# A transformer block's values stage: sums on one engine, stores and loads at other steps, and another split order in the gate pairs

## The chip, the cores and the metric

The kernel runs on one core of one Trainium2 chip. Its time is the device time of one execution in microseconds (us), the median of three runs, with the lowest and the highest beside it. Times of single instructions come from one profiled execution of the same program, which has a time of its own.

The engines are named as in the profile: PE is TensorE's matmul, PEld its weight load, DVE VectorE, ACT ScalarE, POOL GpSimd, and SP the engine that issues most DMAs. ACT and POOL issue DMAs as well, each in the order of its own instructions.

## The reference, cut to what matters

One layer on a residual stream x of 512 tokens by 2048 channels, with 8 attention heads and 8 retention heads of 128 channels each:

```python
h = rmsnorm(x, norm_gain)
proj = h @ w_in
(aq, ak, av, az, iq, ik, iw, rq, rk, rv, rz, ga, gb) = jnp.split(proj, SPLIT_POINTS, axis=-1)
...
a_out = dsa_mixer(aq, ak, av, iq, ik, iw, positions, rel_bias) * jax.nn.silu(az)
...
b_out = retention_mixer(rq, rk, rv, ret_gn_gain) * jax.nn.silu(rz)
merged = jax.nn.sigmoid(ga) * (a_out @ w_a_out) + jax.nn.sigmoid(gb) * (b_out @ w_b_out)
r = x + merged @ w_o
return r + (p_i @ w_ple) * jax.nn.sigmoid(r @ w_ple_gate)
```

The final RMSNorm follows. In `dsa_mixer` an indexer (iq, ik, iw) scores all earlier keys for each token, the 128 best are kept, and softmax attention runs over them with a bias that depends on the distance of two positions. `retention_mixer` rotates rq and rk by position, forms decayed scores within chunks, carries a state from chunk to chunk and normalizes each head. The product of h with w_in is most of the work; its columns are av, rv (1024 each), ga, gb (2048 each), and so on.

## The kernel before, in words

**Numbers in two parts.** The matmuls run in float32r. A weight tile of 128 x 1024 (`wraw`, `wt`) is cut into a high part `wh` (a copy by ACT, line 153, `split_to`) and a low part `wl = wraw - wh` (a subtraction by DVE, line 158). `split_to` queues the ACT copy at once and the subtraction `lag` steps later. Raw tiles are loaded by SP (`load_to`, line 132), some steps earlier. Where a product needs a sum of two weight blocks, a second DMA adds one block onto the raw tile; GpSimd issues it (`add_block`, line 119): for a tile in `in_big` (name `wt`, the attention values' sums) 12 steps after its load, and, for an add that follows a split, right after that split's subtraction. `wh` and `wl` have a few buffers each and `wraw` more, so a split waits for the matmuls that read the buffer's former contents.

**The order of the work.** The kernel writes the instruction order out by hand. After every second or third matmul it calls `step()` (line 181). Each call counts one step, runs what was put off until then by `later(n, f)` (line 175), then one entry of `todo`, or, if that is empty and the step number divides by `state["rate"]`, one entry of the list `bg`. `BG_RATES` (line 1394) gives the rate stage by stage: 2, 3, 5, 24, 16, 8. Every engine takes its instructions in this order, so an ACT instruction that waits holds all later ones of ACT.

**Stages**, in order: norm, rope tables and the indexer's products; the retention values (two calls of `values`, line 744); the attention values (`values_pair`, line 908); then for each head one pair of products for retention (`gate_pair` with `retention(h)`, line 772) and two gate pairs; then pairs for rz, aq and ak, az; at the end attention, the projections, merge and output.

**Seven products in place of eight.** A pair multiplies a 2 x 2 arrangement of blocks by seven products whose inputs are sums of blocks (Strassen's scheme in Winograd's form). `combos` (line 291) makes the seven left inputs from the normalized x, once, for each k from 0 to 7: `sums` (lines 310 to 317) forms four sums of 256 columns, and `parts` (line 297) writes the high part of an input into the left half of a tile (`LO`, ACT) and the low part into its right half (`HI`, line 301, or line 303 where the sign is turned). It is called as `Xh` with `adder` and three of the `low` parts on GpSimd. These calls, the loads and the norm of x (`xn_load`, `xn_norm`, lines 700 and 705) are entries of `bg`; they run while the indexer and the retention values are multiplied. Twelve of the input tiles (`x_away`: the last three products for k below 4) are stored to memory and loaded back in the second call of `values` (`x_load`, line 883, one load for each k from 4 on). The top-k's 48 rounds (line 647), the bias masks (line 659) and the bias products (line 669) are the entries that follow in `bg`; the result of a bias product is copied by ACT and stored from SP, 8 + 4n steps later (`bias_out`, line 689).

**A pair** (`gemm_pair`, line 236) has four PSUM banks p, v, q, r and 14 runs of eight matmuls, high parts over 512 columns and low parts over 256, with a step after every second matmul, so 56 steps. `SPLIT_AT` (line 233) tells ahead of which run which unit (weight tile) of this or the next pair is split; the entry 2: 4 has lag 5, the others 1. The seven units of a pair are, by `block_pair` (line 90), t, w11, w21, w22, t, t, w11; the fifth to seventh use tiles again, after an add.

**Retention.** When the pair's query half and then its key half are done, `rotate(i, o)` (line 783) copies the two halves of `o` into `rb`, swapped (ACT, lines 786 and 787), and multiplies and adds on DVE 3, 5 and 7 steps later; after the keys all further steps of the head are queued, 9 to 94 steps later (lines 875 to 878).

**Values.** `values` accumulates four PSUM tiles of 128 tokens; when they are done, ACT scales each into `rv` (line 764) and stores it (line 892). `values_pair` runs seven products of 16 steps. Its results: ACT copies PSUM to `pv`, `e1`, `e2`, `e3` (`copy`), and `value_out` (line 896) forms a sum `a` on DVE, its high part (ACT) and low part (DVE) two and three steps later, and stores both from ACT's queue 10 and 12 steps later (line 906). After the seventh product `last()` (line 921) calls this for four results at once.

Buffers: 69 tiles of 128 x 512 (`U`), and 5 big ones of 128 x 1280 (`B`: `wt`, `go`, masks).

Of the kernel before, what the change touches and what calls it, by code (L numbers as in the profile page):

```python
# [17 lines left out]
L = 512  # L18
# [17 lines left out]
def block_kernel(tc, xT, pT, posb, posq, w_in, w_v, w_ik, w_a, w_b, w_o, w_ple, w_gate,  # L36
# [4 lines left out]
    with contextlib.ExitStack() as ctx:  # L41
# [29 lines left out]
        raw_tiles = {}  # L71
        unfinished = {}
        state = {"raw": 0, "split": 0, "rate": BG_RATE}
        in_raws, in_big = set(), set()

        def raw(src, k0, nk, cols, plus=None):
            raws.append((src, k0, nk, cols, plus))
# [60 lines left out]
        def split_to(n, lag=1):  # L138
            while state["split"] < min(n, len(units)):
                i = state["split"]  # L140
                load_to(i + 1)
                r, plus, nk, cols = units[i]
                if r in unfinished:
                    unfinished[r]()
                raw = view(raw_tiles[r], nk, cols)
                if i in in_raws:
                    t = wp.tile([128, 2, 512], F32R, name="whl", tag="wraw", bufs=RAW_BUFS)
                    h, l = t[:, 0:1], t[:, 1:2]
                elif nk * cols == L:
# [3 lines left out]
                act.activation(h, raw, AF.Copy)  # L153

                def rest(r=r, plus=plus, l=l, raw=raw, h=h):
                    if unfinished.pop(r, None) is None:
                        return
                    dve.tensor_sub(l, raw, h.bitcast(F32))  # L158
# [71 lines left out]
                for n in ns]  # L230
        RUNS = [(n, part % 2) for n, part in RUNS]

        SPLIT_AT = {0: 3, 2: 4, 3: 4, 4: 5, 7: 6, 8: 7, 10: 8, 12: 9}
        LOAD_AT = (0, 2, 4, 6, 8, 10, 12)

        def gemm_pair(ids, X, done, late=False):
# [35 lines left out]
            for at, (n, part, ks) in enumerate(runs):  # L272
                at = max(at - 4, 0) if late else at
                i, o = ids[n], banks[n]
                if at in SPLIT_AT and not (late and at == 2):
                    split_to(ids[0] + SPLIT_AT[at], 5 if at == 2 else 1)
                if at in LOAD_AT:
                    load_to(ids[LOAD_AT.index(at)] + AHEAD + LOADS)
                w, c = loaded[i][part], (ALL, LO)[part]
                first = ended[n] == 0  # L280
                for k in ks:
                    ended[n] += 1
                    pe.matmul(o[:, c], w[:, k], X[PRODUCTS[n]][k][:, c], start=(n < 4 and first and k == 0),  # L283
                              stop=(ended[n] == 16), skip_group_check=True)
# [6 lines left out]
        def combos(lo, hi, name, keep=None, adder=dve, low={}):  # L291


            X = {n: [None] * 8 for n in PRODUCTS}
# [2 lines left out]
            def parts(n, k, src, sign=1.0):  # L297
                t = U(name + n, F32R)
                act.activation(t[:, LO], src, AF.Copy, scale=sign)
                if sign > 0:  # L300
                    low.get(n, dve).tensor_sub(t[:, HI], src, t[:, LO].bitcast(F32))
                else:
                    dve.scalar_tensor_tensor(t[:, HI], src, sign, t[:, LO].bitcast(F32), op0=OP.mult, op1=OP.subtract)
                dst = keep and keep(n, k)
# [5 lines left out]
            def sums(k):  # L310
                x, y = lo(k), hi(k)
                t1, t2 = T[k] = U("t1"), U("t2")
                adder.tensor_sub(t2[:, LO], x[:, LO], x[:, HI])
                adder.tensor_sub(t1[:, LO], x[:, HI], y[:, HI])
                adder.tensor_sub(t1[:, HI], x[:, LO], t1[:, LO])
                adder.tensor_sub(t2[:, HI], y[:, LO], t1[:, HI])

            def one(k, i):
                if i == 0:
# [302 lines left out]
        def index_tile(m, ix):  # L622
            if m > 1:
                todo.extend(N3)
            for s in range(2):
                for t in range(1, NT):
                    todo.append(lambda s=s, t=t: index_score(2 * m + s, ix[s], t))

        for m in range(2):
            index_tile(m, ix[m])  # L630
        for m in range(2, 8):
# [49 lines left out]
        def bias_out(b, ps):  # L681
# [4 lines left out]
            for n, g in enumerate(gs):  # L686
                dst = bass.AP(tensor=scr.tensor, offset=scr.offset + 16 * (g % 8) * 1280 + TOFF[t],
                              ap=[[1280, 16], [128 * 1280, NH], [1, ln]])
                later(8 + 4 * n, lambda dst=dst, n=n: sp.dma_start(dst, e[:, ln * n:ln * n + ln]))
# [5 lines left out]
        x_away = [(n, k) for k in range(X_AWAY) for n in PRODUCTS[4:]]  # L695
        hd = dp.tile([len(x_away), 128, L], F32, name="hd")
        x_at = {nk: hd[i] for i, nk in enumerate(x_away)}
        xn = {}

        def xn_load(k):  # L700
            for i in (k, k + 8):
                xn[i] = U("xn")
                sp.dma_start(xn[i], xT[:, i, :])

        def xn_norm(k):
            for i in (k, k + 8):
                dve.scalar_tensor_tensor(xn[i], xn[i], ng[:, i:i + 1], R["b"], op0=OP.mult, op1=OP.mult)

        Xh, h_step = combos(lambda k: xn[k], lambda k: xn[k + 8], "h", lambda n, k: x_at.get((n, k)), pool,
                            {n: pool for n in ("s1", "s4", "a22")})  # L710
        bg.append(lambda: xn_load(0))
        for k in range(8):
            if k < 7:
                bg.append(lambda k=k: xn_load(k + 1))
            bg.append(lambda k=k: xn_norm(k))
            bg.extend([lambda k=k, i=i: h_step(k, i) for i in range(X_STEPS)])

        bg.append(lambda: state.update(rate=BG_RATES[1]))
        for r in range(16):
            for t in range(1, NT):  # L720
                bg.append(lambda r=r, t=t: topk_round(t, r == 15))
# [50 lines left out]
        def retention(h):  # L772
# [22 lines left out]
            def queries():  # L795
                E["qt"] = U("qt")
# [84 lines left out]
        x_wanted = collections.deque(x_away)  # L881

        def x_load(s):
            if s >= KT - len(x_away) and x_wanted:
                n, k = x_wanted.popleft()
                Xh[n][k] = U("h" + n, F32R)
                sp.dma_start(Xh[n][k].bitcast(F32), x_at[n, k])

        for i in range(2):
            pss = values(u_rv[i], "rv", x_load if i else lambda s: None)  # L890
            for t, ps in enumerate(pss):
                act.dma_start(rd[i, t], normal(ps, "rv", t))
        state["rate"] = BG_RATES[2]


        def value_out(i, t, f, x, y):

            a = U("av")
            f(a, x, y)
            if t == NT - 1:  # L900
                vs = [(6, a)]
            else:
                h, l = split(a, "av", 2)
                vs = [(2 * t, h.bitcast(F32)), (2 * t + 1, l.bitcast(F32))]
            for j, v in vs:
                later(10 + 2 * (j % 2), lambda j=j, v=v: act.dma_start(vd[i, j], v))

        def values_pair(ids):
            banks = {}
# [4 lines left out]
                for j in range(2):  # L914
                    act.activation(E[n][j], banks[b][j], AF.Copy)

            def out(f, b, n, i, half):
                for j in range(2):
                    value_out(i, 2 * half + j, f, banks[b][j], E[n][j])
# [14 lines left out]
            for n, b in enumerate("vpqrpvp"):  # L934
# [3 lines left out]
                for s, (i, k) in enumerate(seq):  # L938
                    if k == 0:
                        split_to(i + AHEAD)  # L940
                        load_to(i + AHEAD + LOADS)
                    h, l = loaded[i]
                    x = Xh[PRODUCTS[n]][s]
                    for j in range(2):
# [7 lines left out]
                    after[n]()  # L952

        values_pair(u_av)
        state["rate"] = BG_RATES[3]


        sgb, sga, mbs = (dp.tile([16, 128, L], F32, name=n) for n in ("sgb", "sga", "mbs"))
# [26 lines left out]
        state["rate"] = BG_RATES[5]  # L985
        for n, u in enumerate(u_rz):
            y = B("y2")

# [402 lines left out]
AHEAD = 3  # L1391
LOADS = 5
BG_RATE = 4
BG_RATES = (2, 3, 5, 24, 16, 8)
X_AWAY = 4
HEAD = 13
WARM = 10
MANUAL = True
# [96 lines left out]
```

## Time and profile before

| | us |
|---|---|
| time, median of three runs | 1684.4 |
| lowest and highest of the three | 1682.68, 1685.42 |
| the profiled execution's own time | 1680.43 |
| its span in the trace | 1678.7 |

The profile's lines have these forms. A group has line, engine, operation, output<-inputs with partitions x elements and type, then the count, the busy time, the mean in ns of one, and the idle time of the engine ahead of them with what ended most of it. A wait has engine, tile and line, then what released it, with the idle time, the count and the longest. A stretch (`A:B`) has its length, then for PE, PEld, DVE, ACT and POOL the busy time with the number of instructions, then the clock granted to TensorE (1 is full), the share of time the DMA engines were busy, and GB/s. A line of the timeline has the start, the duration, engine, line, operation, tile and count, and in brackets the idle time before it with the releaser. ACTq and SPq mark DMA issues in an engine's queue; SP's issue line gives minimum, median and maximum in ns. The DMA table's last numbers are the count, the size of one and the median time from issue to landing.

### The profile page before, as it was taken

To read this page: it belongs to the slowest core of one execution; us is meant where nothing else is said; L and a number is where in the kernel's file an instruction comes from. 1 tells how busy PE (TensorE), PEld (TensorE's weight loads), DVE (VectorE), ACT (ScalarE), POOL (GpSimd) and SP (SyncE) were. 2 spreads that over 40 slices of the span, in tenths; PEclk is the share of its full clock that TensorE was granted. 3 is DMA by queue.
4 is the path that set the end of the run, shared out by engine and by line. 5 is a ranking of instruction groups with operands and counts; after the bars stand their busy time and mean duration, and the time that the engine had idled before them with its cause. 6 is when DMAs were issued, how large, how long until landed. Compare 5 with 4: busy or idle time off the path is not lost.

```text
span 1678.7 us, 24639 instructions
## 1 busy us (share of the span) xinstructions
PE 1660.2 (99%) x9160; PEld 1441.5 (86%) x9160; DVE 1300.1 (77%) x1984; ACT 880.0 (52%) x1296; POOL 284.3 (17%) x288
## 2 busy tenths in 40 slices
PE   9999999999999999999999999999999999999997
PEld 7988788888888888888888888888888888888896
DVE  7798988988988887887887777787668887864453
ACT  7465544555555555555555555566633445463342
POOL 2116611111111111111331111100000111112222
PEclk9999999999999999999999999999999999999999
DMA  7427989788788788788998888898466788733222
GB/s 288 127 91 236 321 234 268 174 218 218 181 210 220 178 232 230 168 229 227 248 235 219 218 223 218 247 373 284 162 210 193 196 216 218 208 108 101 88 63 101
DMA packets 125577, 343.26 MB, mean 204 GB/s; under 512 B 13713, under 2 KB 25873, under 8 KB 125457
## 3 DMA queue, kind: packets, MB, share of 16 engines
q1 hardware_dynamic: 90400, 235.22, 41.5%
q0 software_dynamic: 23680, 85.99, 28.1%
q10 hardware_dynamic: 11376, 20.47, 3.4%
q8 instruction: 72, 1.18, 0.3%
q14 instruction: 49, 0.39, 0.1%
HBM read 300.21 MB, written 41.42 MB: 204 GB/s over the span
## 4 chain that ended last, share of the span: by engine, by line
PE 89%; DVE 4%; ACT 2%; issue 2%; POOL 2%; DMA 1%; ACTq 0%; SPq 0%; POOLq 0%; DVEq 0%
PE ps_p L283 23%; PE ps_v L283 15%; PE ps_r L283 8%; PE ps_q L283 7%; PE ps_w L213 3%; PE ps_w L214 3%; PE ps_w L215 3%; PE ps_pg L215 3%; PE ps_pg L213 3%; PE ps_pg L214 3%; PE ps_iq L213 1%; PE ps_iq L215 1%; PE ps_iq L214 1%; DVE wl L158 1%; ACT wh L153 1%
## 5 line engine op out<-in xcount | busy, mean ns | idle before, releaser
L158 DVE TENSOR_TENSOR wl<-wraw,wh 128x1024 fp32r<-128x1024 f32 (+2 forms) x459 | 565.4, 1241 | 156.6 <-ACT wh L153 155.4
L153 ACT ACTIVATE wh<-wraw 128x1024 fp32r<-128x1024 f32 (+2 forms) x459 | 474.3, 1043 | 257.9 <-DVE wraw L160 120.3
L119 POOL DMA_DIRECT2D wraw<-w_in x120 | 106.1, 962 | 644.1 <-DVE mk L666 245.3
L283 PE MATMUL ps_p<-hs,wh 128*128 128x512 f32 x640 | 161.1, 394 | 0.0
L246 ACT ACTIVATE e<-ps_p 128x512 f32<-128x512 f32 x144 | 86.1, 598 | 136.7 <-PE ps_p L283 134.3
L283 PEld LDWEIGHTS ps_p<-hs,wh 128*128 128x128 f32 x640 | 114.9, 189 | 21.3 <-issue 0.7
L283 PE MATMUL ps_p<-hs,wl 128*128 128x256 f32 x640 | 92.1, 284 | 1.6 <-DVE wl L158 1.6
L283 PEld LDWEIGHTS ps_p<-hs,wl 128*128 128x128 f32 x640 | 83.0, 192 | 2.1 <-DVE wl L158 2.0
L283 PE MATMUL ps_r<-hs,wh 128*128 128x512 f32 x320 | 79.9, 392 | 1.3 <-ACT wh L153 1.3
L119 POOL DMA_DIRECT2D wraw<-w_o x24 | 21.1, 945 | 348.5 <-DVE wl L158 316.5
L283 PE MATMUL ps_q<-ha,wh 128*128 128x512 f32 x320 | 80.1, 392 | 0.0
L283 PE MATMUL ps_v<-ha,wh 128*128 128x512 f32 x320 | 80.0, 392 | 0.0
L283 PE MATMUL ps_p<-ha,wh 128*128 128x512 f32 x320 | 79.3, 390 | 0.0
L283 PE MATMUL ps_v<-hs,wh 128*128 128x512 f32 x320 | 79.0, 389 | 0.0
L215 PE MATMUL ps_pg<-rh,wl 128*128 128x512 f32 x192 | 74.8, 390 | 0.0
L214 PE MATMUL ps_pg<-rl,wh 128*128 128x512 f32 x192 | 74.7, 389 | 0.0
L213 PE MATMUL ps_pg<-rh,wh 128*128 128x512 f32 x192 | 74.7, 389 | 0.0
L967 DVE TENSOR_TENSOR go<-e_t 128x256 f32<-128x256 f32 x160 | 68.0, 425 | 6.8 <-DMA bd<-go 1.2
L283 PEld LDWEIGHTS ps_r<-hs,wh 128*128 128x128 f32 x320 | 59.6, 188 | 15.8 <-ACT wh L153 2.9
L283 PEld LDWEIGHTS ps_p<-ha,wh 128*128 128x128 f32 x320 | 59.9, 188 | 12.9 <-issue 0.5
L283 PEld LDWEIGHTS ps_v<-hs,wh 128*128 128x128 f32 x320 | 60.1, 188 | 12.5
L283 PEld LDWEIGHTS ps_v<-ha,wh 128*128 128x128 f32 x320 | 59.5, 188 | 12.1
(409 smaller groups left out, 3739.9 us busy)
## 6 DMA issues: line engine op xcount, KB each, us to landing
wraw<-w_in SPq DMA_DIRECT2D x172, 512.0 KB, 5.3
wraw<-w_in POOLq DMA_DIRECT2D x120, 512.0 KB, 8.0
wraw<-w_v SPq DMA_DIRECT2D x32, 512.0 KB, 4.2
wraw<-w_o SPq DMA_DIRECT2D x32, 512.0 KB, 4.8
wraw<-w_o POOLq DMA_DIRECT2D x24, 512.0 KB, 7.0
wraw<-w_gate SPq DMA_DIRECT2D x24, 512.0 KB, 4.0
wraw<-w_b SPq DMA_DIRECT2D x16, 512.0 KB, 5.9
wraw<-w_a SPq DMA_DIRECT2D x16, 512.0 KB, 4.1
```

Source lines behind the costliest of these rows:

```text
L119: pool.dma_start(out=view(raw_tiles[r], nk, cols), in_=src[:, k0:k0 + nk, :], accum_op=OP.add)
L153: act.activation(h, raw, AF.Copy)
L158: dve.tensor_sub(l, raw, h.bitcast(F32))
L213: pe.matmul(o, h[:, k, w], a, start=(s == order[0]), stop=False)
L214: pe.matmul(o, h[:, k, w], b, start=False, stop=False)
L215: pe.matmul(o, l[:, k, w], a, start=False, stop=(s == order[-1]))
L246: act.activation(E[n], src, AF.Copy)
L283: pe.matmul(o[:, c], w[:, k], X[PRODUCTS[n]][k][:, c], start=(n < 4 and first and k == 0), stop=(ended[n] == 16), skip_group_check=True)
L967: dve.tensor_add(o[:, q], c0, c1)
```

## The change

1. `combos` has no `adder` and no `low`: all sums and low parts are made by DVE. The calls themselves stay entries of `bg`, now built by `x_steps(k)`; the code that defines them stands earlier in the program.
2. Behind them four empty entries stand in `bg` where a change of rate stood, and `BG_RATES` loses its 3.
3. The stores of `rv` are put off: tile t's scaling and store come 3t steps after the product's end.
4. The first add onto a big `wt` tile after its split comes `ADD_LAG` = 24 steps later.
5. The twelve loads back follow `X_BACK`: six in the second retention value call (k = 4, 6, ..., 14), six in `values_pair` (the first product's seventh k, four in the second product, one at the start of the third).
6. `value_out` takes the steps at which the high part, the low part and the stores come. For the four results of `last()` they start 2, 6, 10 and 16 steps after the end, with 6, 9 and 22 (and 26 for the low part's store) behind each; the three that have parts keep sum, high and low part in one big buffer (`avhl`), and their stores alternate between ACT's and GpSimd's queue.
7. `SPLIT_AT` splits the fourth unit ahead of run 1, with lag 9, instead of ahead of run 2 with lag 5.
8. `rotate` for the keys (i = 1) does everything 4 steps later, the swap too; the head's further steps come 6 steps later.
9. The bias stores go out from GpSimd's queue, 14 + 4n steps after the copy.

```diff
-                        add_block(r, plus)
+                        later(ADD_LAG if r in in_big and r not in added else 0, lambda: add_block(r, plus))
+                        added.add(r)
...
-        SPLIT_AT = {0: 3, 2: 4, 3: 4, 4: 5, 7: 6, 8: 7, 10: 8, 12: 9}
+        SPLIT_AT = {0: 3, 1: 4, 3: 4, 4: 5, 7: 6, 8: 7, 10: 8, 12: 9}
...
-                if at in SPLIT_AT and not (late and at == 2):
-                    split_to(ids[0] + SPLIT_AT[at], 5 if at == 2 else 1)
+                if at in SPLIT_AT and not (late and at == 1):
+                    split_to(ids[0] + SPLIT_AT[at], 9 if at == 1 else 1)
...
-                    low.get(n, dve).tensor_sub(t[:, HI], src, t[:, LO].bitcast(F32))
+                    dve.tensor_sub(t[:, HI], src, t[:, LO].bitcast(F32))
...
-                adder.tensor_sub(t2[:, LO], x[:, LO], x[:, HI])
...
+                dve.tensor_sub(t2[:, LO], x[:, LO], x[:, HI])
...
-                later(8 + 4 * n, lambda dst=dst, n=n: sp.dma_start(dst, e[:, ln * n:ln * n + ln]))
+                later(14 + 4 * n, lambda dst=dst, n=n: pool.dma_start(out=dst, in_=e[:, ln * n:ln * n + ln]))
...
-        Xh, h_step = combos(lambda k: xn[k], lambda k: xn[k + 8], "h", lambda n, k: x_at.get((n, k)), pool,
-                            {n: pool for n in ("s1", "s4", "a22")})
...
-        bg.append(lambda: state.update(rate=BG_RATES[1]))
...
-        bg.append(lambda: state.update(rate=BG_RATES[4]))
+        bg.extend([lambda: None] * 4)
+        bg.extend(rounds)
+        bg.append(lambda: state.update(rate=BG_RATES[3]))
...
-                act.activation(b[0:64, :], o[64:128, :], AF.Copy)
-                act.activation(b[64:128, :], o[0:64, :], AF.Copy)
-                later(3, lambda: dve.tensor_mul(o, o, ct))
-                later(5, lambda: dve.tensor_mul(b, b, st))
-                later(7, lambda: dve.tensor_add(o, o, b))
+
+                def swap():
+                    act.activation(b[0:64, :], o[64:128, :], AF.Copy)
+                    act.activation(b[64:128, :], o[0:64, :], AF.Copy)
+
+                n = 4 * i
+                later(n, swap)
+                later(n + 3, lambda: dve.tensor_mul(o, o, ct))
+                later(n + 5, lambda: dve.tensor_mul(b, b, st))
+                later(n + 7, lambda: dve.tensor_add(o, o, b))
                 if i:
                     for n, f in steps:
-                        later(n, f)
+                        later(n + 6, f)
...
-            if s >= KT - len(x_away) and x_wanted:
+            if s in X_BACK:
...
-            for t, ps in enumerate(pss):
-                act.dma_start(rd[i, t], normal(ps, "rv", t))
+                later(3 * t, lambda i=i, t=t, ps=ps: act.dma_start(rd[i, t], normal(ps, "rv", t)))
...
-            a = U("av")
+            def store(j, v):
+                (pool if big and j % 2 else act).dma_start(out=vd[i, j], in_=v)
+
+            if big and t < NT - 1:
+                b = B("avhl", F32R)
+                a, l, h = b[:, 0:L].bitcast(F32), b[:, 0:L], b[:, L:2 * L]
+            else:
+                a = U("av")
             f(a, x, y)
             if t == NT - 1:
-                vs = [(6, a)]
-            else:
-                h, l = split(a, "av", 2)
-                vs = [(2 * t, h.bitcast(F32)), (2 * t + 1, l.bitcast(F32))]
-            for j, v in vs:
-                later(10 + 2 * (j % 2), lambda j=j, v=v: act.dma_start(vd[i, j], v))
+                return later(lags[2], lambda: store(6, a))
+            if not big:
+                h, l = U("avh", F32R), U("avl", F32R)
+            later(lags[0], lambda: act.activation(h, a, AF.Copy))
+            later(lags[1], lambda: dve.tensor_sub(l, a, h.bitcast(F32)))
+            later(lags[2], lambda: store(2 * t, h.bitcast(F32)))
+            later(lags[2] + 4, lambda: store(2 * t + 1, l.bitcast(F32)))
...
-                out(dve.tensor_sub, "p", "pv", 1, 1)
-                out(dve.tensor_add, "r", "e3", 1, 0)
+                out(dve.tensor_sub, "p", "pv", 1, 1, (2, 6), (6, 9, 22), True)
+                out(dve.tensor_add, "r", "e3", 1, 0, (10, 16), (6, 9, 22), True)
...
+                    x_load(KT + 8 * n + s)
...
-BG_RATES = (2, 3, 5, 24, 16, 8)
+BG_RATES = (2, 5, 24, 16, 8)
+ADD_LAG = 24
 X_AWAY = 4
+X_BACK = (4, 6, 8, 10, 12, 14, 22, 24, 26, 28, 30, 32)
```

More of the change, by code (lines that the diff above doesn't have):

```diff
@@ L289, in gemm_pair, with combos @@
                     after[n]()
-        def combos(lo, hi, name, keep=None, adder=dve, low={}):
+        def combos(lo, hi, name, keep=None):
             X = {n: [None] * 8 for n in PRODUCTS}
@@ L627, in index_tile, with xn_load, xn_norm, x_steps @@
                     todo.append(lambda s=s, t=t: index_score(2 * m + s, ix[s], t))
+        x_away = [(n, k) for k in range(X_AWAY) for n in PRODUCTS[4:]]
+        hd = dp.tile([len(x_away), 128, L], F32, name="hd")
+        x_at = {nk: hd[i] for i, nk in enumerate(x_away)}
+        xn = {}
+        def xn_load(k):
+            for i in (k, k + 8):
+                xn[i] = U("xn")
+                sp.dma_start(xn[i], xT[:, i, :])
+        def xn_norm(k):
+            for i in (k, k + 8):
+                dve.scalar_tensor_tensor(xn[i], xn[i], ng[:, i:i + 1], R["b"], op0=OP.mult, op1=OP.mult)
+        Xh, h_step = combos(lambda k: xn[k], lambda k: xn[k + 8], "h", lambda n, k: x_at.get((n, k)))
+        def x_steps(k):
+            load = [lambda: xn_load(k + 1)] if k < 7 else []
+            return load + [lambda: xn_norm(k)] + [lambda i=i: h_step(k, i) for i in range(X_STEPS)]
         for m in range(2):
@@ L915, in copy, with out @@
                     act.activation(E[n][j], banks[b][j], AF.Copy)
-            def out(f, b, n, i, half):
+            def out(f, b, n, i, half, at=(0, 0), *rest):
                 for j in range(2):
-                    value_out(i, 2 * half + j, f, banks[b][j], E[n][j])
+                    later(at[j], lambda j=j: value_out(i, 2 * half + j, f, banks[b][j], E[n][j], *(rest or ((2, 3, 10),))))
             def last():
                 copy("e3", "p")
-                out(dve.tensor_sub, "p", "pv", 1, 1)
-                out(dve.tensor_add, "r", "e3", 1, 0)
+                out(dve.tensor_sub, "p", "pv", 1, 1, (2, 6), (6, 9, 22), True)
+                out(dve.tensor_add, "r", "e3", 1, 0, (10, 16), (6, 9, 22), True)
             after = {
```

38 lines of the change are left out of this document (11 added, 27 removed).

## The prediction, made before the changed kernel was run

> **What bounds the kernel now.** I read the engines' shares first, then the list of TensorE's waits, then the busy time of the stretches in which it waits, then the chain of waits for the length of a run of eight matmuls.
>
> ```profile
> span 1678.7 us, 24639 instructions
> PE 1660.2 (99%) x9160; PEld 1441.5 (86%) x9160; DVE 1300.1 (77%) x1984; ACT 880.0 (52%) x1296; POOL 284.3 (17%) x288
> ...
> PE ps_p L283 <- DVE wl L158: 1.6, 2, 1.3
> PE ps_vv L948 <- DVE wl L158: 1.5, 2, 0.8
> PE ps_vv L947 <- ACT wh L153: 1.4, 1, 1.4
> PE ps_r L283 <- ACT wh L153: 1.3, 3, 0.6
> ```
>
> TensorE is the bound: 18.5 us of the span are not matmul, and the change adds and takes away no matmul. All it can win is waits. The list names them: each is for a weight tile's high part (wh, made by ACT) or low part (wl, made by VectorE). These windows hold them:
>
> ```profile
> 190.00:200.00 10.00, 7.91 (x34) 5.86 (x32) 6.63 (x9) 7.05 (x14) 6.57 (x9) 1.00 1.05 365
> 200.00:210.00 10.00, 9.16 (x39) 7.39 (x40) 9.81 (x17) 5.53 (x8) 1.76 (x2) 1.00 1.06 276
> 280.00:290.00 10.00, 8.70 (x53) 7.63 (x52) 6.91 (x11) 6.03 (x8) 0.00 (x0) 1.00 1.02 346
> 300.00:310.00 10.00, 9.38 (x61) 8.01 (x60) 9.81 (x14) 5.42 (x9) 0.00 (x0) 1.00 0.56 145
> 360.00:370.00 10.00, 9.73 (x67) 8.66 (x66) 9.62 (x16) 4.25 (x6) 0.00 (x0) 1.00 0.70 154
> 485.00:490.00 5.00, 4.60 (x28) 3.80 (x28) 4.72 (x8) 2.54 (x4) 0.21 (x1) 1.00 0.99 178
> 495.00:500.00 5.00, 4.67 (x28) 3.91 (x28) 4.93 (x7) 3.29 (x5) 0.00 (x0) 1.00 0.35 120
> ...
> 320.90 0.95 PE ps_v L283 x8
> 322.81 1.84 PE ps_q L283 x8
> L283 PE MATMUL ps_q<-ha,wh 128*128 128x512 f32 x320 | 80.1, 392 | 0.0
> ```
>
> Behind the length stand the busy times of PE, PEld, DVE, ACT and POOL. A matmul is drawn 0.39 us long, but they follow each other every 0.23 (1.84/8), so each wait hides 0.16 more than PE's idle time. Idle plus 0.16 per wait: **A**, the start of the attention values' product (190 to 210), 2.93 + 3 x 0.16 = 3.4; **B**, 280 to 290, 1.30 + 0.16 = 1.46; **C**, 300 to 310, 0.62 + 0.16 = 0.78; **D**, 360 to 370, 0.43; **E**, 485 to 490 and 495 to 500, 0.56 and 0.49. Together 7.1 us. About 0.2% of the time, 3.4 us, is what a measurement of this kernel can tell from no change; twice that is the most to be won.
>
> **The change, part by part.**
>
> *Sums and low parts from GpSimd to VectorE (combos), and A.* Per k, seven 256-column operations move. First what VectorE does from 100 to 205 us today, then the same operations where GpSimd is idle:
>
> ```profile
> L158 DVE TENSOR_TENSOR wl<-wraw,wh 128x1024 fp32r<-128x1024 f32 x15 | 22.8, 1518 | 6.9 <-ACT wh L153 6.9
> L707 DVE SCALAR_TENSOR_TENSOR xn<-xn,g_sb,r_b 128x512 f32<-128x512 f32 x16 | 15.0, 980 | 0.0
> L301 DVE TENSOR_TENSOR hs<-t,hs 128x256 fp32r<-128x256 f32 x16 | 13.9, 890 | 0.0
> L303 DVE SCALAR_TENSOR_TENSOR ha<-xn,ha 128x256 fp32r<-128x256 f32 x8 | 7.9, 990 | 0.0
> L301 DVE TENSOR_TENSOR ha<-xn,ha 128x256 fp32r<-128x256 f32 x8 | 7.1, 889 | 0.0
> L158 DVE TENSOR_TENSOR wl<-wt,wh 128x1024 fp32r<-128x1024 f32 x4 | 5.5, 1364 | 4.0 <-ACT wh L153 4.0
> ...
> L301 DVE TENSOR_TENSOR hs<-t,hs x16: 411/958/964, 117.7 to 193.7; 128x256 fp32r<-128x256 f32 x16
> 107.63 1.41 DVE L707 SCALAR_TENSOR_TENSOR xn<-xn,g_sb,r_b 128x512 f32<-128x512 f32 x2
> 1239.05 0.42 DVE L313 TENSOR_TENSOR t<-sm 128x256 f32<-128x256 f32 x1
> 1242.99 0.68 DVE L1176 TENSOR_TENSOR sm<-ps_w,sm 128x512 f32<-128x512 f32 x1
> ...
> 197.87 0.69 ACT L764 ACTIVATE rv<-ps_vn,r_nat 128x512 f32<-128x512 f32 x1 [0.48 <-POOL hs L301]
> 198.59 0.33 ACTq L892 DMA_DIRECT2D rd<-rv  x1
> 198.97 2.01 ACT L153 ACTIVATE wh<-wt 128x1024 fp32r<-128x1024 f32 x2 [0.40 <-ACT rv L764]
> 200.05 1.22 DVE L158 TENSOR_TENSOR wl<-wt,wh 128x1024 fp32r<-128x1024 f32 x1 [3.39 <-ACT wh L153]
> ```
>
> A 256-column subtraction takes VectorE 0.96 us (median) here, 0.42 in the later stage in which GpSimd computes nothing: the two hold each other up. In that later stage the eleven operations of one k (4 sums, 7 low parts) take 1242.99 - 1239.05 = 3.94 us; two norms take 1.41. VectorE's sum today: 15.0 + 13.9 + 7.9 + 7.1 = 43.9 for eight k, and 22.8 + 5.5 = 28.3 for 19 low parts of weights. Changed: 8 x (3.94 + 1.41) = 42.8, and 19 x 1.22 = 23.2. So VectorE is given seven more operations per k and has 6.2 us *less* to do, and no sum goes by way of GpSimd. A k has 12 steps of three matmuls, 36 x 0.23 = 8.3 us, for 5.35 + 1.5 x 1.22 = 7.2 us of VectorE, 87%: no backlog.
>
> A itself: ACT, late from its waits on GpSimd, makes four evictions with their stores, 4 x (0.69 + 0.33) = 4.1 us, ahead of wh; VectorE stands 3.39 us. Changed, three of the four come 3, 6 and 9 steps later, behind wh. I take 3.3 of the 3.4 us (bounds 0 and 3.4). The first add into a `wt` tile goes out 24 steps (16.6 us) later, and six of the twelve loads back move behind the retention values. Both are wanted by the fifth product, four products of 16 steps on; that covers them, at nothing. If it didn't, wh would wait for a DMA: a rival below.
>
> *Results in big buffers, stores late, and B.*
>
> ```profile
> 278.32 2.81 ACTq L906 DMA_DIRECT2D vd<-avl  x3
> 283.24 1.23 DVE L158 TENSOR_TENSOR wl<-wraw,wh 128x1024 fp32r<-128x1024 f32 x1 [2.99 <-ACT wh L153]
> ```
>
> ACT's queue stands in stores whose data VectorE still makes; wh waits behind them, VectorE then idles 2.99 us, then PE waits. Changed, the last product's results are formed 2 to 16 steps after its end and stored 22 and 26 steps after that, half of them from GpSimd's queue: neither queue stands. B's 1.46 goes whole (bounds 0 and 1.46), and VectorE has its 2.99 us back, which serves C.
>
> *Fourth product split a run sooner, keys' rotation four steps later (C, D, E).*
>
> ```profile
> 300.04 1.06 ACT L153 ACTIVATE wh<-wraw 128x1024 fp32r<-128x1024 f32 x1
> 494.12 1.22 DVE L158 TENSOR_TENSOR wl<-wraw,wh 128x1024 fp32r<-128x1024 f32 x1
> ```
>
> After a retention pair ACT waits for VectorE's last `go`, swaps the halves (rb), and only then makes the fourth product's wh, which ends at 301.10 as PE goes on. Changed, wh is queued ahead of the swap and waits only for the first run's matmuls. D goes (0.43); of C's 0.78 I take 0.6, since wl may be late in its place. It is in E: the second wait there is for the low part at 494.12, and VectorE's operations up to it stay the same ones, so what wh gives back is lost at wl: 0 (bounds 0 and 1.05). The retention's later steps all move 6 steps on together, so their distances stay.
>
> *Rounds of the top-k.* Four idle entries replace the rate change; the rounds end two rounds (48 steps) later, in the pairs. The same operations under VectorE's slack: nothing, with bounds of E's 0.49 won or twice that lost.
>
> *Bias stores from GpSimd's queue.*
>
> ```profile
> L689 SPq DMA_DIRECT2D scr<-bev x32: 518/587/2042, 553.0 to 1051.5; - x32
> DMA to landing us min/median/max: 2.4/4.4/11.2
> L119 POOL DMA_DIRECT2D wraw<-w_in x120: 857/883/1207, 258.3 to 1079.9; - x120
> wraw<-w_in POOLq DMA_DIRECT2D x120, 512.0 KB, 8.0
> 600.00:800.00 200.00, 200.00 (x1231) 175.51 (x1230) 163.89 (x253) 112.58 (x147) 29.09 (x31) 1.00 0.82 211
> ```
>
> SP is relieved of 32 x 0.59 us on which nothing waited (PE is busy 200.00 of 200.00 there): no gain. GpSimd's issue isn't shown for this shape; the nearest row is 0.88 each. Two together put 1.8 us in front of an add into a weight tile. That add follows the first unit's split, at step 41 of a pair, and is wanted by the fifth unit's in the next. In runs of 1.84 and 0.95 us that is 5.1 us to the pair's end, and 11.2 of the next less wh (1.06) and wl (1.22), 8.9: 14.0, less wl 1.22, issue 0.88 and landing 8.0, leaves 3.9 us. 1.8 fits: 0 (bounds 0 and the rival's 25).
>
> **The sum**: 3.3 + 1.46 + 0.6 + 0.43 = 5.8 us off the profiled execution's 1680.4 (span 1678.7 and 1.7 around it), 1674.6. The three timed runs have their median 4.0 above it, at 1684.4; carried over, **1678.6**.
>
> **Rivals.** *VectorE takes the place.* It is busy 9.81 of 10 us in 300 to 310. If the two later rounds and the spread results use up the 2.99 us, C, D and half of A stay: 5.8 - 0.6 - 0.43 - 1.65 = 3.1 won, 1681.3. Against it: that idle time lies right ahead of C. 0.16.
> *The change doesn't do what it says*, because transfers are late: DMA shares of 1.05 and 1.06 around A (the column before the last) leave nothing for a PE that comes sooner. A stays, 5.8 - 3.3 = 2.5 won, 1681.9. Against it: in the waits above it is never a DMA that releases PE. 0.08.
> *Slower, by GpSimd's queue.* Should a pair of stores hold the next add more than 3.9 us, PE waits at the fifth unit in each of the 11 places where bias banks go out. Issue 1.8 and the stores' own passage in the one software queue, bounded by SP's median landing of 4.4, make 6.2: 2.3 us each, 25 at worst; in half of the places 12.7 - 5.8 = 6.9 lost, 1691.3. It decides from 3.9 us on. 0.14.
>
> The Trainium skill speaks for this rival ("SBUF — State Buffer", section "SBUF: two separate sides"): while VectorE runs an operation through both its ports, GpSimd can't write descriptors, and a DMA of 0.62 us took 3.1. By that figure, an estimate, two stores hold the queue 6.2 us. The trace doesn't bear it out: no issue of the 120 took over 1.21 us, though 128 mask operations of VectorE, of one SBUF input each, run among them.
>
> ```profile
> L666 DVE TENSOR_SCALAR mk<-relf,thr x128: 275/410/1461, 502.3 to 1039.4; 128x512 f16<-128x512 f32 x32, 128x384 f16<-128x384 f32 x32, 128x256 f16<-128x256 f32 x32, 128x128 f16<-128x128 f32 x32
> ```
>
> **Numbers.** Forecast 0.62 (a gain of 3.4 to 9 us), the two small cases 0.24, slower 0.14. The range 1675.5 to 1685.5 goes from 8.9 us won (all 7.1 and some of what the timed runs lie above the profiled one) to 1.1 lost; outside are the slower case and little else. Faster 0.62, same 0.24, slower 0.14.
>
> **What would show it.** No tensor operation of GpSimd between 108 and 198; hs on VectorE at 0.42 us; no PE wait on ps_vv; vd stores of ACT and GpSimd that wait for nothing; wh ahead of rb after each retention pair; bias stores of about 0.9 us on GpSimd. I am wrong if PE waits at ps_p for wl after the first retention pairs, if wh waits for a DMA of w_in between 550 and 1080, or if the values' waits stand where they were.

## The result, and the profile after

The changed kernel takes **1677.15 us** (median of 6 runs, 1674.79 to 1678.00) against 1683.24 for the kernel before beside it (median of 6, 1682.11 to 1685.42): a ratio of **0.996, 95% interval 0.9947 to 0.9973**, so 6.1 us less. The forecast was 1678.6. Its profiled execution took 1677.63 us, near its own median; that of before, 1680.43, was faster than any of that kernel's six timed runs. Profile against profile only 2.8 us are gone, and the experiments explain both figures.

The head of the page of the changed kernel:

```profile
span 1675.9 us, 24609 instructions
...
PE 1660.5 (99%) x9160; PEld 1441.8 (86%) x9160; DVE 1296.1 (77%) x2040; ACT 879.4 (52%) x1296; POOL 250.7 (15%) x267
```

TensorE's waits in the changed kernel (tile and line, releaser; total, times, longest):

```profile
PE ps_r L284 <- DVE wl L158: 1.3, 2, 0.9
PE ps_p L284 <- DVE wl L158: 1.2, 3, 0.6
...
PE ps_r L284 <- ACT wh L153: 0.3, 1, 0.3
```

Both waits of ps_vv are gone, and so is most of ps_r's waiting for wh. But wl now holds ps_r and ps_p five times. The same stretches as before, in the changed kernel:

```profile
190.00:200.00 10.00, 10.00 (x46) 8.28 (x45) 4.93 (x9) 5.60 (x7) 2.62 (x3) 1.00 1.06 302
200.00:210.00 10.00, 10.00 (x46) 8.29 (x45) 7.30 (x13) 5.33 (x6) 0.00 (x0) 1.00 1.04 337
280.00:290.00 10.00, 10.00 (x55) 8.63 (x54) 9.52 (x14) 5.13 (x8) 2.36 (x4) 1.00 1.06 371
300.00:310.00 10.00, 10.00 (x60) 8.86 (x59) 9.72 (x14) 7.24 (x10) 0.87 (x1) 1.00 0.61 181
360.00:370.00 10.00, 9.62 (x65) 8.56 (x64) 9.71 (x15) 4.41 (x7) 0.00 (x0) 1.00 0.47 152
485.00:490.00 5.00, 4.13 (x26) 3.54 (x25) 4.69 (x9) 2.83 (x5) 0.00 (x0) 1.00 0.76 125
```

PE (second figure) is full at A, B and C: 3.5 + 1.46 + 0.79 = 5.8 us won, counted at the matmuls that waited. At D and E it still stands. From the starts of the runs of eight, wl makes TensorE late by 0.26 and 0.44 us at 361 to 363, 0.56 and 0.72 at 424 to 427, 1.03 and 0.52 at 489 to 492, and 0.28 at 552: 3.8 us, two of them too short for the list. A wait for wh at 946 adds 0.5. Together 4.3, where D and E had cost 1.5: 2.8 us lost again. These sums leave out that the matmuls right behind a wait come some 0.1 us late too. From one matmul to the same matmul of the other kernel, 6.4 us are won up to C and 4.1 lost behind it.

Where the lateness begins is seen one pair earlier, on SyncE. Waits of ScalarE and of SyncE's queue between 300 and 560 us, first before the change, then after:

```profile
ACT wh L153 <- DMA wraw<-w_in: 1.3, 1, 1.3
...
SPq L873 <- ACT yT L872: 23.8, 4, 5.9
```

```profile
ACT wh L153 <- DMA wraw<-w_in: 12.9, 8, 2.5
...
SPq L878 <- ACT yT L877: 35.9, 4, 9.5
```

SyncE's queue stands at the store of a head's retention result (yT) until that exists: 12 us longer in four heads. Behind the store stand three weight loads, and eight wh now wait for a weight's DMA. One head, in SyncE's queue and with TensorE's first run of the pair in which the waits fall; before, then after:

```profile
456.35 0.33 SPq L873 DMA_DIRECT2D yd<-yT  x1
456.72 1.95 SPq L132 DMA_DIRECT2D wraw<-w_in  x3
...
481.89 1.98 PE L283 MATMUL ps_v<-hs,wh 128*128 128x512 f32 x8
```

```profile
454.29 0.33 SPq L878 DMA_DIRECT2D yd<-yT  x1
454.66 1.38 SPq L132 DMA_DIRECT2D wraw<-w_in  x3
...
477.88 1.98 PE L284 MATMUL ps_v<-hs,wh 128*128 128x512 f32 x8
```

The store was 25.5 us ahead of that pair and is 23.6 us ahead now: 1.9 us later, for the 6 steps. Between the loads and wh stands one more link, GpSimd's adds onto weight tiles, before and after:

```profile
460.26 0.92 POOL L119 DMA_DIRECT2D wraw<-w_in  x1 [11.15 <-DVE wl L158]
462.52 1.78 POOL L119 DMA_DIRECT2D wraw<-w_in  x2 [1.34 <-DVE wl L158]
```

```profile
455.37 0.91 POOL L119 DMA_DIRECT2D wraw<-w_in  x1 [10.14 <-DVE wl L158]
458.08 0.87 POOL L119 DMA_DIRECT2D wraw<-w_in  x1 [1.79 <-DVE m L671]
460.54 0.86 POOL L119 DMA_DIRECT2D wraw<-w_in  x1 [1.60 <-DMA wraw<-w_in]
```

The third add now waits for a load to land, the one issued at 454.66, just behind the store. By the landings in the trace the three adds take 11.4, 12.5 and 13.6 us (8.5, 9.4 and 12.6 before the change) and land at 466.81, 470.61 and 474.18, 2.1 to 2.7 us later against the pair's first run. All eight waits of wh are for such adds; here wh at 466.83 waits for the first and at 474.26 for the third. That the first two take longer because the loads now run beside them is likely, but was not tried alone. The chain goes on in the changed kernel through ScalarE, VectorE and TensorE:

```profile
466.83 1.06 ACT L153 ACTIVATE wh<-wraw 128x1024 fp32r<-128x1024 f32 x1 [2.48 <-DMA wraw<-w_in]
474.26 2.01 ACT L153 ACTIVATE wh<-wraw 128x1024 fp32r<-128x1024 f32 x2 [1.26 <-DMA wraw<-w_in]
...
475.35 1.22 DVE L158 TENSOR_TENSOR wl<-wraw,wh 128x1024 fp32r<-128x1024 f32 x1 [0.48 <-ACT wh L153]
487.78 1.22 DVE L158 TENSOR_TENSOR wl<-wraw,wh 128x1024 fp32r<-128x1024 f32 x1
...
489.06 0.98 PE L284 MATMUL ps_r<-hs,wl 128*128 128x256 f32 x6 [0.87 <-DVE wl L158]
```

The low part at 475.35 starts 2.5 us ahead of the pair's first run; its counterpart before the change, at 478.10, started 3.8 ahead:

```profile
478.10 1.23 DVE L158 TENSOR_TENSOR wl<-wraw,wh 128x1024 fp32r<-128x1024 f32 x1 [1.24 <-ACT wh L153]
```

VectorE is 1.3 us behind. In the 12 us up to 487.78 it has a top-k round, two rotations, the sums of three results and two more low parts to make, and can't catch up: the wl of 487.78 ends at 489.00, and TensorE stood for it.

### The profile page after: what moved, and what is told of

Its sections match the earlier page's. It is cut to its first block, busy times and chain, and to the rows that moved or that the text cites. A ratio compares the mean times of both kernels' runs of the same rounds, so it can differ in the third digit from the quotient of the medians.

```text
span 1675.9 us, 24609 instructions
## 1 busy us (share of the span) xinstructions
PE 1660.5 (99%) x9160; PEld 1441.8 (86%) x9160; DVE 1296.1 (77%) x2040; ACT 879.4 (52%) x1296; POOL 250.7 (15%) x267
## 4 chain that ended last, share of the span: by engine, by line
PE 91%; DVE 4%; ACT 2%; DMA 1%; issue 1%; POOL 0%; SPq 0%; ACTq 0%; DVEq 0%; POOLq 0%
PE ps_p L284 23%; PE ps_v L284 15%; PE ps_r L284 7%; PE ps_q L284 7%; PE ps_w L215 3%; PE ps_w L216 3%; PE ps_w L214 3%; PE ps_pg L216 3%; PE ps_pg L215 3%; PE ps_pg L214 3%; PE ps_vn L755 2%; PE ps_vn L756 2%; PE ps_vn L757 2%; PE ps_iq L214 1%; PE ps_iq L216 1%; PE ps_iq L215 1%
```

## The experiments

Times are medians of the timed runs, and each ratio is to the kernel before, run beside it on the same chip. Theory **Q**: SyncE's queue, as just read. Rival **V**: the keys' rotation, now right ahead of the fourth product's wl on VectorE. Rival **R**: the top-k rounds, two later.

| run | edit | us | ratio, 95% interval |
|---|---|---|---|
| changed | | 1677.15 | 0.9960 (0.9947 to 0.9973) |
| e1 | yT stored from ScalarE | 1672.44 | 0.9944 (0.9930 to 0.9958) |
| e2 | rotation and steps unmoved | 1673.22 | 0.9949 (0.9937 to 0.9962) |
| e3 | also the old split order | 1673.71 | 0.9951 (0.9939 to 0.9964) |
| e4 | kernel before | 1682.46 | 0.9999 (0.9991 to 1.0008) |
| e5 | rotation moved, steps not | 1672.42 | 0.9939 (0.9927 to 0.9952) |
| e6 | e1, results at once | 1675.11 | 0.9959 (0.9946 to 0.9971) |
| e7 | e1, sums on GpSimd | 1672.68 | 0.9939 (0.9925 to 0.9953) |
| e8 | e1, rv stores at once | 1672.93 | 0.9942 (0.9929 to 0.9954) |
| e9 | e1, both of e7 and e8 | 1677.81 | 0.9972 (0.9964 to 0.9981) |
| e10 | e1, bias stores on SyncE | 1672.64 | 0.9948 (0.9935 to 0.9962) |
| e11 | e1 with e5, no empty entries | 1672.34 | 0.9948 (0.9935 to 0.9960) |
| e12 | changed kernel again | 1675.81 | 0.9966 (0.9954 to 0.9979) |

### e1: the store of yT from ScalarE's queue

```diff
-                    later(2, lambda: sp.dma_start(yd[h], E["yT"]))
+                    later(2, lambda: act.dma_start(yd[h], E["yT"]))
```

> The changed kernel, with one edit: each head's retention result yT is stored from ScalarE's queue instead of SyncE's. Theory Q (SyncE's queue): in the changed kernel the store of yT stands 6 steps later in SyncE's queue, ahead of three weight loads, so these land late, wh waits for them (8 waits, 12.9 us between 300 and 560), wl follows late, and TensorE's new waits for wl (0.26, 0.44, 0.56, 0.72, 1.03, 0.52, 0.28 = 3.8 us between 360 and 553) come from there. It expects that ScalarE's waits for a DMA of w_in nearly go, that at most 1 us of the 3.8 is left, and a time 2.5 to 3.5 us under the changed kernel's, some 1674 us. Rival V (VectorE): the keys' rotation, 4 steps later, now stands right ahead of the fourth product's wl on VectorE. It expects that the 3.8 us stay within 0.5, whatever the loads do, and the time of the changed kernel, 1677.

1672.44. What is left of TensorE's waits in the pairs, and ScalarE's longest waits for wh between 300 and 560:

```profile
PE ps_p L284 <- DVE wl L158: 0.4, 2, 0.2
...
ACT wh L153 <- DVE wraw L160: 22.8, 8, 4.2
ACT wh L153 <- PE ps_p L284: 21.0, 4, 5.5
```

No row of that list names a DMA of w_in any more, and of 3.8 us of wl waits two of 0.33 and 0.38 are left. One DMA issue on another queue is worth 3.4 to 4.7 us (against 1675.81 in e12 and 1677.15), where Q expected 2.5 to 3.5; VectorE's order was not touched. In the head shown, the three adds land in 8.2, 8.5 and 11.4 us again. Q holds, V and R fall as main cause.

### e2 and e3: the parts of the pairs taken back

```diff
-                n = 4 * i
+                n = 0
...
-                        later(n + 6, f)
+                        later(n, f)
```

> The changed kernel, with the keys' rotation and the retention's later steps put back to where they were (no 4 and no 6 steps); the fourth product's split stays a run sooner. Theories Q and V both expect that the wl waits at 360 to 553 (3.8 us) go; Q in addition that the wh waits for a DMA of w_in fall from 8 to 2 or fewer between 300 and 560, V says nothing of these. Both leave open whether wh then stands behind the swap of the keys' halves on ScalarE again, as before the change (0.4 to 0.8 us a head): without it 1674, with it 1676.

1673.22, lower than either figure expected. The wl waits are gone. wh stands behind the swap again, in two pairs and by 0.44 us each (start to start), and the waits of wh for a weight's DMA are two:

```profile
PE ps_r L284 <- ACT wh L153: 0.6, 2, 0.3
...
ACT wh L153 <- DMA wraw<-w_in: 1.5, 2, 1.1
```

e3 has this edit and also

```diff
-        SPLIT_AT = {0: 3, 1: 4, 3: 4, 4: 5, 7: 6, 8: 7, 10: 8, 12: 9}
+        SPLIT_AT = {0: 3, 2: 4, 3: 4, 4: 5, 7: 6, 8: 7, 10: 8, 12: 9}
...
-                    split_to(ids[0] + SPLIT_AT[at], 9 if at == 1 else 1)
+                    split_to(ids[0] + SPLIT_AT[at], 5 if at == 2 else 1)
```

> The changed kernel, with the split order and the rotation both as before the change: what is left of the change is the values stage and the bias stores. Q and V expect the waits of the kernel before in the pairs (0.8 + 0.4 + 0.6 + 0.5 = 2.3 us for wh and one wl between 300 and 500) and none at 190 to 290: 1.5 us better than the changed kernel in the profile, about 1675.6. Rival R (top-k rounds, two later by the empty entries): the new wl waits come from the rounds on VectorE and stay in this run, 1677 or more.

1673.71, lower than expected: with the old pairs only 0.61 and 0.45 us of wh waits are there, at 295 and 484, not the 2.3 of before.

```profile
PE ps_r L284 <- ACT wh L153: 0.7, 2, 0.5
```

D and the wl wait of E are gone without any edit of the pairs. What moved them there (the rounds are two later, and VectorE comes out of the values stage earlier) was not taken apart. R falls once more: the rounds are as late here. So the values stage with the bias stores and the empty entries brings 8.7 us (1682.41 to 1673.71), and the pairs' part, as the change has it, takes back 2 to 3.5 (to 1677.15, or 1675.81 in e12).

### e4: the kernel before, as a control

> The kernel before, unchanged, as a control of the comparison. Expected: ratio 1.000 within 0.0015, and in its profile the same waits A to E, 7.1 us. Its first profile was 4 us under the median of its timed runs, while the changed kernel's profile lay at its own median; if this profile comes at 1683 or so, it shows where those 2 to 3 us lie.

The ratio is 0.9999, and the profiled execution took 1683.06, 2.6 over the first profile. Waits A to E are all there. B is longer, and the granted clock (third figure from the end) is not 1:

```profile
PE ps_p L283 <- DVE wl L158: 2.8, 2, 2.4
...
201.50:202.00 0.50, 0.50 (x2) 0.40 (x3) 0.47 (x3) 0.40 (x1) 0.38 (x1) 0.50 1.13 311
202.00:204.00 2.00, 2.00 (x6) 1.56 (x5) 2.00 (x3) 0.00 (x0) 0.55 (x2) 0.50 1.04 293
...
202.33 0.63 PE L947 MATMUL ps_vv<-wh,hs 128*128 128x512 f32 x1
202.76 0.63 PE L948 MATMUL ps_vv<-wl,hs 128*128 128x512 f32 x1
```

B is 2.59 us from start to start, 1.46 in the first profile. And in A's last wait the clock drops to half for some 3.4 us: matmuls follow each other every 0.43 us in place of 0.23. From the first matmul of ps_vv to the first of the pairs it takes 81.6 us here, 80.0 in the first profile, 76.2 in the changed kernel. A thus costs 3.8 or 5.4 us, as the clock falls. From this profile to that of e3, 9.2 us are gone: 5.4 at A, 2.6 at B, and 1.2 for C to E and the rest.

### e5: the rotation 4 steps later, the rest in its old place

```diff
-                        later(n + 6, f)
+                        later(n, f)
```

> The changed kernel, with the retention's later steps put back by 6 (so the store of yT has its old place in SyncE's queue); the keys' rotation stays 4 steps later. Theory Q (SyncE's queue): the lateness comes from the 6 steps, not from the rotation's 4. It expects at most 2 waits of wh for a DMA of w_in between 300 and 560, no wait of TensorE above 0.4 us in the pairs, and 1672 to 1673. Rival V (the rotation stands ahead of the fourth product's wl on VectorE) is tried here with the rotation alone: it expects at least 1.5 us of wl waits between 360 and 553, and 1674 to 1676.

1672.42, and

```profile
ACT wh L153 <- DMA wraw<-w_in: 0.9, 1, 0.9
```

No wait of TensorE in the pairs is over 0.28 us. The rotation's 4 steps do no harm; the 6 steps of the rest did. Q holds, V falls.

### e6: the values' last results at once

```diff
-                out(dve.tensor_sub, "p", "pv", 1, 1, (2, 6), (6, 9, 22), True)
-                out(dve.tensor_add, "r", "e3", 1, 0, (10, 16), (6, 9, 22), True)
+                out(dve.tensor_sub, "p", "pv", 1, 1)
+                out(dve.tensor_add, "r", "e3", 1, 0)
```

> The kernel of e1_yd_from_act, with the last four results of the values formed at once and stored from ScalarE's queue 10 and 14 steps later, in small buffers, as before the change (there 10 and 12). The prediction's part B: ScalarE's queue stands in the stores, wh is late, and the wait for wl at 280 to 290 (1.46 in the first profile of before, 2.6 in the control's) comes back: 1673.9 to 1675.0, against e1's 1672.4. Rival: VectorE, relieved in stage A, no longer makes the results late, and the stores find their data: nothing comes back, 1672.4 within 0.6.

1675.11 (1673.98 to 1677.86), 2.7 over e1. ScalarE's queue is taken up by the stores, and wl is late:

```profile
273.89 2.14 ACTq L903 DMA_DIRECT2D vd<-avl  x3
...
PE ps_r L284 <- DVE wl L158: 0.3, 1, 0.3
```

The profile, the fastest of the five, shows 0.46 us of it (start to start), at 298 and not at 285. So the edit is worth more than nothing, and its price varies from run to run; the long B wait itself did not come back in this profile.

The stores do not wait for VectorE, neither here nor in the kernel before, where the three low parts are done at 279.12:

```profile
277.23 1.89 DVE L735 TENSOR_TENSOR avl<-av,avh 128x512 fp32r<-128x512 f32 x3
```

Their stores are issued at 278.32, 279.02 and 280.05, each after its low part was done, and it is the issues that are long: 0.60, 0.99 and 1.08 us, where the first of the seven in a row takes 0.33 (in e4 up to 1.23, in e6 up to 0.92). In the changed kernel none of ScalarE's takes over 0.67. Why they grow stays open.

### e7, e8 and e9: the two causes of A

e7 gives `sums` and the low parts of s1, s4 and a22 to `pool` again; e8 has

```diff
-                later(3 * t, lambda i=i, t=t, ps=ps: act.dma_start(rd[i, t], normal(ps, "rv", t)))
+                later(0, lambda i=i, t=t, ps=ps: act.dma_start(rd[i, t], normal(ps, "rv", t)))
```

and e9 has both.

> The kernel of e1_yd_from_act, with the sums and the low parts of s1, s4 and a22 on GpSimd again. The prediction's part A: GpSimd and VectorE hold each other up, so VectorE's 256-column operations go back from 0.42 to about 0.96 us, and 1 to 3.5 us of the waits at 195 to 202 come back: 1673.5 to 1676. Rival: the waits there came from the four evictions and their stores, which stood ahead of wh; these are spread here, so less than 0.5 comes back, 1672.4 to 1672.9.

> The kernel of e1_yd_from_act, with the four evictions of the retention values and their stores right at the product's end, as before the change. The prediction's part A has this as its second cause: wh waits behind 3 x 1.0 us of ScalarE, so 1 to 1.6 us of the waits at 195 to 202 come back, 1673.5 to 1674. Rival: with VectorE free the first wh is made early enough, and nothing comes back: 1672.4 within 0.5.

> The kernel of e1_yd_from_act, with both edits of stage A taken back at once: the sums and three low parts on GpSimd, and the retention values' evictions and stores right at the product's end. Theory B2 (two causes, each curable alone): in e7 and e8 either edit alone kept the waits at 195 to 202 away; with both gone the waits come back, 2 us or more in the profile and 1675 to 1678. Rival X (the loads back, spread in this kernel, or the empty entries were the cure): the waits stay away, 1672.4 to 1673.2.

e7 takes 1672.68 and e8 1672.93: neither brings a wait of ps_vv back, though in e7 VectorE's subtractions are as slow as before (group of lines, 100 to 205 us; first e7, then e8):

```profile
L302 DVE TENSOR_TENSOR hs<-t,hs 128x256 fp32r<-128x256 f32 x16 | 13.7, 872 | 0.2 <-ACT hs L300 0.2
```

```profile
L302 DVE TENSOR_TENSOR hs<-t,hs 128x256 fp32r<-128x256 f32 x32 | 11.8, 416 | 0.0
```

e9 takes 1677.81, 5 us more, and A is back whole, with the halved clock:

```profile
PE ps_vv L960 <- ACT wh L153: 1.6, 1, 1.6
PE ps_vv L961 <- DVE wl L158: 1.3, 2, 0.8
...
203.00:204.00 1.00, 1.00 (x3) 0.72 (x3) 1.00 (x1) 0.00 (x0) 0.49 (x1) 0.50 1.09 252
```

The first of the second product's four evictions shows how each cure acts: at 191.27 us in e7, at 189.52 in e8, at 194.30 in e9 (194.54 before the change):

```profile
191.27 0.67 ACT L764 ACTIVATE rv<-ps_vn,r_nat 128x512 f32<-128x512 f32 x1
```

```profile
189.52 0.69 ACT L764 ACTIVATE rv<-ps_vn,r_nat 128x512 f32<-128x512 f32 x1 [0.82 <-PE ps_vn L757]
```

```profile
194.30 0.67 ACT L764 ACTIVATE rv<-ps_vn,r_nat 128x512 f32<-128x512 f32 x1
```

ScalarE comes 3 us sooner to the evictions when the first product's stores are spread, 5 when nothing goes by way of GpSimd, and either is enough. Theory B2 holds. The spread loads (in e9 as in the changed kernel) are not what cured A.

### e10: the bias stores from SyncE's queue

```diff
-                later(14 + 4 * n, lambda dst=dst, n=n: pool.dma_start(out=dst, in_=e[:, ln * n:ln * n + ln]))
+                later(8 + 4 * n, lambda dst=dst, n=n: sp.dma_start(dst, e[:, ln * n:ln * n + ln]))
```

> The kernel of e1_yd_from_act, with the bias stores from SyncE's queue again, 8 + 4n steps after the copy. The prediction costed this part at nothing, and feared GpSimd's queue. Theory N (nothing): 1672.4 within 0.5, no wait of TensorE between 550 and 1080 that e1 doesn't have. Rival Q2: as with the store of yT, a bias store that waits for bev holds the weight loads behind it on SyncE, wh waits for a DMA of w_in more than in e1, and the time is 1673 or more.

1672.64: nothing, and no new wait in the pairs (its profile took 1674.73, with a wait of 1.8 us for the first weights at 10 us, which is at most 1.0 in the other profiles). The bias stores' issues in the changed kernel, from GpSimd:

```profile
L710 POOL DMA_DIRECT2D scr<-bev x32: 530/788/1171, 570.3 to 1067.7; - x32
```

### e11: what is left, together

This is e1 with the edit of e5 and without `bg.extend([lambda: None] * 4)`.

> The kernel of e1_yd_from_act, with the retention's later steps put back by 6 as in e5 and without the four empty entries ahead of the top-k rounds. Theory Q has nothing left on SyncE's queue that is late; what remains in e1 and e5 are waits for wl of 0.2 to 0.4 at 425 and 488, beside a top-k round each. Expected: these move or go with the rounds, 1671.5 to 1672.4. Rival V (the rotation ahead of wl) expects them to stay, 1672.4.

1672.34; one wl wait of 0.21 us, at 362 instead of 425 and 488. It moved with the rounds. e1, e5 and e11 can't be told apart; each is about 10 us under the kernel before and 3.4 to 4.8 under the changed one.

### e12: the changed kernel again

> The changed kernel itself, on the same chip as the three above, as a control. Expected: 1677 within 1.5, the waits for wl between 360 and 553 again (3.8 us in the first profile), each after a wait of wh for a DMA of w_in, none at 195 to 290.

1675.81 (1675.13 to 1676.05; e11 on the same chip 1671.47 to 1674.12). The waits for wl are at five of the seven places, 2.7 us in all, and wh waits for a DMA six times:

```profile
ACT wh L153 <- DMA wraw<-w_in: 9.4, 6, 2.3
```

## Why the prediction was right, and where it was not

The direction and the time were right, but the time came out of two errors of opposite sign. The profile was to lose 5.8 us, and 4.0 were added for the timed runs. It lost 2.8, and the changed kernel's profile lies 0.5 above its median.

- **A**, taken at 3.3: 3.5 at the matmuls that waited, 3.8 over the stretch. The causes were named rightly, but as a sum; e7 to e9 show two causes of which curing either was enough. That VectorE has 6.2 us less to do was wrong: the same groups take 46.6 + 25.7 = 72.3 us after the change, and took 72.2. The changed side had been reckoned from start to start (0.36 us an operation) and the side before by busy time (0.42).
- **B**, 1.46: gone in the profile. That ScalarE's stores hold wh is supported by e6, which doesn't show the whole of it. But the stores do not stand for data "VectorE still makes", as the prediction has it: the data was there, and the issues themselves were long.
- **C**, taken at 0.6: 0.79. With the old split order and rotation (e3) 0.61 of it stays, with the new split order and the old rotation (e2) 0.44, with both new (e5) none: wh had to come ahead of the swap, as predicted.
- **D**, 0.43 to go, and **E**, nothing: this failed. The step was "The retention's later steps all move 6 steps on together, so their distances stay." Their distances from each other stay, but the last of them is a store in SyncE's queue, and its distance from the weight loads behind it does not. wh is queued ahead of the swap as predicted, but the loads go out 1.9 us later, and the adds that wh waits for land 2.1 to 2.7 later. At D and behind it the change costs 2.8 us net at the matmuls that waited, 4.1 with those behind them; e1 and e5 take nearly all of that away in two ways. That D would go by the split is not shown either: it is gone in e3, without the split.
- Two of the signs that were to show an error came: waits at ps_p for wl after the retention pairs, and wh waiting for a DMA of w_in between 550 and 1080, 16.1 us in 12 waits, where it was 1.3 in 2. The second was meant for the bias stores on GpSimd's queue, but these are not its cause: it falls to 2.1 us when the 6 steps are taken back (e5), and is 6.4 in e1 and 6.8 in e10 with and without the bias stores on GpSimd. TensorE lost only 0.5 us to it. That the lateness hurts it mostly before 560 goes with the rounds, which fill VectorE until 508; no run tests this.
- **The 4.0 us carried over** were taken as a constant. With six runs the median is 1683.24, 2.8 above the first profile. In e4's profile, 2.6 above the first, they belong to the waits: with A's the clock can fall to half (1.6 us), and B's was 1.46 or 2.59. Both went with the waits. That the forecast came within 1.5 us is luck: errors of 3.0 us in the profile and 4.5 in what was carried over cancelled.
- **Rounds and bias stores** at nothing: right for the bias stores (e10); the rounds were tried only together with other edits (e3, e11). No bias store's issue on GpSimd took over 1.17 us, the median was 0.79 where 0.88 was taken, and the slower case did not come. The price of 3.1 us for a DMA, from the Trainium skill ("SBUF — State Buffer", section "SBUF: two separate sides"), is not seen in these issues.
- The first add of a `wt` tile, 24 steps later, and the loads back were not tried alone. The changed kernel shows no wait of TensorE at the values' later products.

## What to carry to other kernels

When steps are moved, follow each DMA among them to its queue, and ask what stands behind it: here a store that waits for its data held the later loads of its queue, and the price appeared a pair later on another engine. A wait can have two causes of which either cure is enough, so test each alone and both together before one gets the credit. Here a profile faster than all the timed runs didn't lie a constant below them: look for waits whose length, or whose effect on the clock, changes from run to run.

## What the runs showed of the hardware that was not expected

In two of the three profiles that have A's waits (e4 and e9, not the first one) the granted clock fell to 0.50, from 201.2 and 202.3 us on, for some 3.4 us, though the longest single wait was 1.6 us. It costs about 1.6 us: eight matmuls in 3.45 us instead of 1.84. None of the profiles without these waits shows it there, and e3's timed runs lie within 0.8 us where those of before spread over 5. Of the 50 timed runs of the kernel before in the experiments, 23 have a mean granted clock of 0.996 or less; of the 50 runs of e1 to e3, e5 to e8 and e10 to e12, none has. The Trainium skill ("TensorE: Matmul & The Clock Gate", section "Part 1: The HAM clock gate (the "warmup" mystery)") has the half rate follow an idle window of about 3.4 us, a window that runs free of the kernel; the length of the half rate agrees, but here waits of 1.4 and 0.8 us with little work between them came ahead of it. Why the first profile, with the same waits, keeps the full clock is not shown.

DMA issues grew on one queue: of seven in a row from ScalarE the first took 0.33 us and the last 1.08 (1.10 in e4), though their data was there.
